# The third and fourth hidden tile of the first SwiGLU as a pair of seven block products

## The chip, the cores and the metric

The kernel runs on one core of a Trainium2 chip. The metric is device time in microseconds (us), the median over runs of the same kernel. In the profile, PE is TensorE (PEld its weight loads), DVE is VectorE, ACT is ScalarE, POOL is GpSimd, and SP is the engine whose queue issues the DMAs.

## The reference

One decoder layer on 512 tokens of width 1024, in float32. What the change touches is the first of its two SwiGLU blocks:

```
def swiglu(x, w_gate, w_up, w_down):
    return (jax.nn.silu(x @ w_gate) * (x @ w_up)) @ w_down

h = h + 0.5 * rms_norm(swiglu(rms_norm(h, ffn1_pre_g), ffn1_w_gate, ffn1_w_up, ffn1_w_down), ffn1_post_g)
u = rms_norm(h, mix_pre_g)          # then two token mixers: sparse latent attention and a gated recurrence
h = h + rms_norm(merged @ w_out, mix_post_g)
h = h + 0.5 * rms_norm(swiglu(...), ffn2_post_g)   # the second SwiGLU, its own weights
h = h + rms_norm(sigmoid(rms_norm(h) @ w_ple_gate) * (p @ w_ple_proj), ple_post_g)
```

The hidden width is 2816, that is 22 tiles of 128.

## The kernel before, in words

Activations lie with channels on the 128 partitions and the 512 tokens along the free dimension. Every float32 operand is split into a rounded part ("hi", cast by ACT) and the remainder ("lo", a subtraction on DVE), and every product is three matmuls: hi by hi, lo weight by hi, hi weight by lo. All matmuls are issued at line 259.

A SwiGLU (`ffn`) goes through its 22 hidden tiles in four groups, given by `GROUPS` as (first tile, tiles, how many of them are plain). The hidden tiles of a group are made first, and then all 8 output tiles get the group's share of the down product. A plain tile takes 24 matmuls for its gate and 24 for its up product, each over all 512 tokens. The other tiles go in pairs (`pair`, lines 512 to 590). There the product of a pair of weight tiles with the input is seen as a 2 by 2 block product (two tiles by two halves of the input channels, two halves of the channels by two halves of the tokens), and the gate and the up side each do it with seven block products instead of eight, in the order of `SEVEN` (lines 27 and 28):

```
SEVEN = (("a", True, "A11", "B11"), ("b", True, "A12", "B21"), ("a", False, "S2", "T2"), ("c", True, "S1", "T1"),
         ("a", False, "S3", "T3"), ("c", False, "S4", "B22"), ("a", False, "A22", "T4"))
```

The first name is the bank that is added into, the B's are quarters of the input, the A's of the weights, the S's sums of weight quarters. Each block product is 4 steps of 3 matmuls over 256 tokens. A pair's weight sums are made by POOL (lines 532 and 536) and DVE (533, 539, 565), and each is split by ACT (508) and DVE (509).

The T's are sums of input quarters. `input_sums` (lines 481 to 492) makes them once per SwiGLU. It is a generator of four steps; step k covers one of four channel blocks for all four T's: two scaled copies on ACT (486), four subtractions in a row on POOL (490), and a split of each result on ACT and DVE (199, 200, tile name T). Before, in the first SwiGLU, two steps are taken after tile 0, one after tile 1 and one after tile 2.

In the first SwiGLU tile 0 is special: `start` brings its weights and the input in together, and `start_scale` makes the factor R of the RMS norm (matmuls at 273 and 283, powers on POOL at 248, copies at 315). `hidden` then takes a product times R (382), a Silu on ACT (389), the product of both (391) and a split into hid_hi and hid_lo (199, 200).

Buffers come from pools: 5 raw weight tiles (`raw`), 6 split ones (`w`), 6 work tiles (`t`), and 6 PSUM banks that are handed out in turn (mm, pl, mm, pl, pt, po). A scheduler puts the instructions of each engine into a fixed order when the program is built, and each engine then works through its own queue in that order, waiting for what an instruction needs. A weight tile's DMA waits until its raw buffer is free.

Of the kernel before, what the change touches and what calls it, by code (L numbers as in the profile page):

```python
# [19 lines left out]
FT = DFF // P  # L20
EPS = 1e-6

GROUPS = ((0, 4, 4), (4, 6, 0), (10, 6, 0), (16, 6, 0))
INNER = 6


# [54 lines left out]
class Layer:  # L81
# [312 lines left out]
    def ffn(self, name, nxt, y, pool, spill=None, begin=None):  # L394
        nc, a = self.nc, self.a
        wg, wu, wd = (a[f"{name}_w_{s}"] for s in ("gate", "up", "down"))
        post = self.ghalf[f"{name}_post"]
        hid_hi = pool.tile([P, INNER, NT], F32R, name="hid_hi")
        hid_lo = pool.tile([P, INNER, NT], F32R, name="hid_lo")
        acc = self.accum(NT)  # L400
        for f0, nf, plain in GROUPS:
            first, last = f0 == 0, f0 + nf == FT
            j0 = 0
            if first and not begin:
                j0 = 3
                w = [self.first_weights(name, (wg[j], wu[j]), D, shift=SHIFT) for j in range(j0)]

                tags = iter(("mm", "mm", "pl", "pl", "pt", "po"))
                for cols in HALF:
                    for js in ((0, 1), (2,)):  # L410
                        banks = [self.bank(next(tags)) for _ in js]
                        ps = [(b[:, :256], b[:, 256:]) for b in banks]
                        self.mm3s([x for j, b in zip(js, ps) for x in zip(b, w[j])], self.hg_hi, self.hg_lo, KT, cols,
                                  shared=True)
                        for j, b in zip(js, ps):
                            self.hidden(hid_hi, hid_lo, j, *b, cols)
            elif first:
                j0 = 1
                w = begin[0](wg[0], wu[0])
                ps = self.bank("pl"), self.bank("pt")  # L420
                self.mm3s(list(zip(ps, w)), self.hg_hi, self.hg_lo, KT, FULL)
                begin[1]()
                self.hidden(hid_hi, hid_lo, 0, *ps, FULL)
            if first:
                sums = self.input_sums(f"{name}_pre", pool)
                next(sums)
                next(sums)
            for j in range(j0, plain):
                pg, pu = self.bank(), self.bank()
                self.mm3(pg, self.weight(wg[f0 + j], D), self.hg_hi, self.hg_lo, KT, FULL)  # L430
                self.mm3(pu, self.weight(wu[f0 + j], D), self.hg_hi, self.hg_lo, KT, FULL)
                self.hidden(hid_hi, hid_lo, j, pg, pu, FULL)
                next(sums, None)
            if first:
                for _ in sums:
                    pass
            for j in range(plain, nf, 2):
                self.pair(pool, [src[f0 + j:f0 + j + 2] for src in (wg, wu)], hid_hi, hid_lo, j)
            w = {}

            def parts(m, ps, cols, ks):
                if m not in w:
                    w[m] = self.weight(wd[m][:, f0 * P:(f0 + nf) * P], nf * P)
                for k in ks:
                    self.mm3_step(k, ps, w[m], hid_hi, hid_lo, nf, cols)

            def store(m, ps, cols):
                if first:
                    nc.scalar.copy(y[:, m, cols], ps)
                else:  # L450
                    nc.vector.tensor_tensor(y[:, m, cols], y[:, m, cols], ps, op=OP.add)
                if last:
                    self.square_sum(acc[:, cols], y[:, m, cols], m == 0, nc.vector if m == KT - 1 else nc.gpsimd)

            def product(m, cols):
                ps = self.bank()[:, :cols.stop - cols.start]
                parts(m, ps, cols, range(nf))
                store(m, ps, cols)


            early = 3
            ps = [self.bank() for _ in range(early)]
            for ks in (range(nf - 2), range(nf - 2, nf)):
                for m in range(early):
                    parts(m, ps[m], FULL, ks)
            for m in range(early):
                store(m, ps[m], FULL)
            if last:
                self.last_product(product, y, acc, post, nxt, TURN[name], spill, early, self.e)
                if begin:  # L470
                    self.ple_proj(pool)
            else:
                for m in range(early, KT):
                    product(m, FULL)
                if first and begin:
                    begin[2]()
# [799 lines left out]
```

## Time and profile before

| what | value |
|---|---|
| median of 3 runs | 1225.35 us (1225.05 to 1231.47) |
| the profiled execution | 1224.83 us |
| its span, first to last instruction | 1223.0 us |
| PE busy | 1185.8 us, 97% of the span |
| DVE busy | 896.9 us, 73% |
| ACT busy | 658.4 us, 54% |
| POOL busy | 521.5 us, 43% |

Times below are counted from the start of the span. A busy share is an average over all stages. For a change in one stage the stretch of that stage counts: here the first 85 us, in which the first group of the first SwiGLU runs.

### The profile page before, as it was taken

The page shows a single profiled execution, that of the slowest core. Times are in us where ns is not written, and L with a number is a line of the kernel's source. Part 1 is how long each engine was busy: PE and PEld are TensorE (multiplying, and loading weights), DVE is VectorE, ACT ScalarE, POOL GpSimd, SP SyncE. Part 2 cuts the span into 40 slices and gives each one's busy share as a digit, 9 for nine tenths or more (in the row PEclk, how much of TensorE's full clock was granted, in tenths as well). Part 3 has the DMA queues.
Part 4 walks back from the last instruction along what each step waited for, and adds up shares of the span by engine and source line. Part 5 has one row for each costly group of instructions (what it writes and reads, how often), then busy time and mean ns, then how long its engine had stood idle before and what let it go on. Part 6 is the DMA issues. An engine that isn't in the chain of part 4 may idle for free.

```text
span 1223.0 us, 20125 instructions
## 1 busy us (share of the span) xinstructions
PE 1185.8 (97%) x7580; PEld 1064.7 (87%) x7580; DVE 896.9 (73%) x1496; ACT 658.4 (54%) x1193; POOL 521.5 (43%) x521
## 2 busy tenths in 40 slices
PE   7999999999999999998999999999999999999997
PEld 6889899999999887787788878898899899899976
DVE  8769669669757479998576748387787587588396
ACT  6655435435645464564677755456655265255263
POOL 3525235235153213645657642363452252253364
PEclk9999999999999999999999999999999999999999
DMA  7242522522635212323222236322234233233131
GB/s 253 62 130 66 170 77 65 164 83 65 197 128 180 96 52 70 129 87 100 66 94 91 74 104 213 105 61 65 92 108 126 68 117 122 71 117 119 59 138 70
DMA packets 47058, 130.23 MB, mean 106 GB/s; under 512 B 5400, under 2 KB 9840, under 8 KB 46960
## 3 DMA queue, kind: packets, MB, share of 16 engines
q1 hardware_dynamic: 46960, 128.95, 32.2%
q8 instruction: 59, 0.97, 0.3%
q14 instruction: 39, 0.32, 0.1%
HBM read 118.16 MB, written 10.77 MB: 105 GB/s over the span
## 4 chain that ended last, share of the span: by engine, by line
PE 65%; DVE 16%; ACT 5%; POOL 5%; issue 5%; DMA 2%; SPq 0%; DVEq 0%; POOLq 0%; ACTq 0%
PE mm L259 24%; PE pl L259 18%; PE pt L259 8%; PE po L259 8%; DVE sc L706 2%; DVE w L178 2%; DVE w L509 1%; DVE small L705 1%; DVE hg_lo L306 1%; PE po L755 1%; DMA g<-gate_d 1%; DVE h L360 1%; DVE z L358 1%; POOL t L490 1%; POOL acc L299 1%
## 5 line engine op out<-in xcount | busy, mean ns | idle before, releaser
L259 PE MATMUL mm<-hg_hi,w 128*128 128x512 f32 (+1 forms) x984 | 268.1, 355 | 3.3 <-ACT hg_hi L199 1.5
L259 PEld LDWEIGHTS mm<-hg_hi,w 128*128 128x128 f32 x984 | 171.0, 188 | 27.8 <-ACT hg_hi L199 1.7
L176 ACT ACTIVATE w<-raw 128x1024 fp32r<-128x1024 f32 (+5 forms) x146 | 131.9, 910 | 84.6 <-PE pl L259 26.0
L259 PE MATMUL mm<-hg_lo,w 128*128 128x512 f32 (+1 forms) x492 | 173.4, 353 | 0.1
L178 DVE TENSOR_TENSOR w<-raw,w 128x1024 fp32r<-128x1024 f32 (+5 forms) x132 | 141.3, 1075 | 40.4 <-ACT w L176 40.3
L532 POOL TENSOR_TENSOR s<-raw 128x512 f32<-128x512 f32 x36 | 50.8, 1411 | 238.3 <-DMA raw<-ffn_w_gate 164.3
L509 DVE TENSOR_TENSOR w<-raw,w 128x1024 fp32r<-128x1024 f32 (+1 forms) x108 | 132.0, 1236 | 7.2 <-ACT w L508 6.5
L508 ACT ACTIVATE w<-raw 128x1024 fp32r<-128x1024 f32 (+1 forms) x108 | 95.3, 911 | 45.4 <-PE mm L259 15.0
L259 PE MATMUL pl<-hg_hi,w 128*128 128x256 f32 (+1 forms) x520 | 111.6, 307 | 5.0 <-ACT w L176 5.0
L259 PEld LDWEIGHTS mm<-hg_lo,w 128*128 128x128 f32 x492 | 92.3, 188 | 12.0 <-DVE hg_lo L306 0.3
L299 POOL TENSOR_TENSOR acc<-acc,sq 128x256 f32<-128x256 f32 x78 | 68.0, 879 | 72.3 <-ACT sq L298 70.9
L259 PEld LDWEIGHTS pl<-hg_hi,w 128*128 128x128 f32 x520 | 84.2, 191 | 10.0 <-ACT w L176 5.0
L259 PE MATMUL pl<-hg_lo,w 128*128 128x256 f32 (+1 forms) x260 | 79.1, 304 | 0.7 <-DVE hg_lo L306 0.7
L259 PE MATMUL pl<-T,w 128*128 128x256 f32 x576 | 75.5, 281 | 4.1 <-ACT sq L548 4.1
L259 PE MATMUL pl<-hid_hi,w 128*128 128x512 f32 (+1 forms) x276 | 76.6, 362 | 0.0
L259 PE MATMUL mm<-T,w 128*128 128x256 f32 x576 | 74.9, 279 | 1.5 <-ACT sq L548 1.5
L562 POOL TENSOR_TENSOR t<-t,acc 128x256 f32<-128x256 f32 x36 | 43.1, 1198 | 75.8 <-ACT t L561 75.8
L259 PEld LDWEIGHTS pl<-T,w 128*128 128x128 f32 x576 | 70.9, 190 | 4.7 <-ACT sq L548 4.7
L533 DVE TENSOR_TENSOR s<-s,raw 128x512 f32<-128x512 f32 x36 | 39.0, 1084 | 47.9 <-POOL s L532 47.9
L259 PE MATMUL mm<-hid_hi,w 128*128 128x512 f32 (+1 forms) x268 | 73.4, 361 | 0.0
L259 PEld LDWEIGHTS mm<-T,w 128*128 128x128 f32 x576 | 70.4, 189 | 1.7 <-ACT sq L548 1.7
L508 ACT ACTIVATE w<-s 128x1024 fp32r<-128x1024 f32 x36 | 38.3, 1064 | 56.8 <-PE pl L259 18.7
(361 smaller groups left out, 3009.8 us busy)
## 6 DMA issues: line engine op xcount, KB each, us to landing
raw<-ffn_w_gate SPq DMA_DIRECT2D x43, 512.0 KB, 3.9
raw<-ffn_w_up SPq DMA_DIRECT2D x43, 512.0 KB, 4.1
raw<-ffn_w_down SPq DMA_DIRECT2D x48, 384.0 KB, 3.7
raw<-w_gates SPq DMA_DIRECT2D x16, 512.0 KB, 3.6
raw<-ffn_w_down SPq DMA_DIRECT2D x16, 256.0 KB, 2.7
gate_d<-t SPq DMA_DIRECT2D x16, 256.0 KB, 2.1
raw<-w_br SPq DMA_DIRECT2D x8, 512.0 KB, 3.5
raw<-w_out SPq DMA_DIRECT2D x8, 512.0 KB, 4.0
```

What stands on the lines that cost most here:

```text
L176: hi = nc.scalar.activation(w[:, 0, c], raw[:, c], AF.Copy)
L178: lo = eng.tensor_tensor(w[:, 1, c], raw[:, c], w[:, 0, c].bitcast(F32), op=OP.subtract)
L259: i = self.nc.tensor.matmul(*args, **kw)
L299: eng.tensor_tensor(acc[:, c:c + 256], acc[:, c:c + 256], sq, op=OP.add)
L306: lo = nc.vector.scalar_tensor_tensor(self.hg_lo[:, k, cols], self.h[:, k, cols], g, self.hg_hi[:, k, cols].bitcast(F32), op0=OP.mult, op1 ...
L358: nc.vector.scalar_tensor_tensor(z, y[:, k, c], g[:, k:k + 1], bc, op0=OP.mult, op1=OP.mult)
L508: self.nc.scalar.activation(w[:, 0], raw, AF.Copy)
L509: eng.tensor_tensor(w[:, 1], raw, w[:, 0].bitcast(F32), op=OP.subtract)
L532: pool_.tensor_tensor(s[:, low], r[1][:, low], r[1][:, high], op=OP.add)
L533: dve.tensor_tensor(s[:, high], s[:, low], r[0][:, low], op=OP.subtract)
L562: pool_.tensor_tensor(o2[:, two], o2[:, two], k["P5"], op=OP.add)
L706: nc.vector.match_replace(sc, best, sc, TAKEN)
```

## The change

`GROUPS` becomes a table by SwiGLU. The second SwiGLU keeps its numbers. In the first one, two of the first group's four tiles are plain instead of four, so tiles 2 and 3 go as a pair, and all four steps of `input_sums` are taken after tile 0 instead of two. One more line moves every line number behind it by one in the changed kernel.

```
-GROUPS = ((0, 4, 4), (4, 6, 0), (10, 6, 0), (16, 6, 0))
+GROUPS = {"ffn1": ((0, 4, 2), (4, 6, 0), (10, 6, 0), (16, 6, 0)),
+          "ffn2": ((0, 4, 4), (4, 6, 0), (10, 6, 0), (16, 6, 0))}
...
-        for f0, nf, plain in GROUPS:
+        for f0, nf, plain in GROUPS[name]:
...
                 sums = self.input_sums(f"{name}_pre", pool)
-                next(sums)
-                next(sums)
+                for _ in range(2 if plain > 2 else 4):
+                    next(sums)
```

The scheduler makes a new order of it. On DVE, between the weights of tile 1 and the hidden values of tile 0, there stood before (w is a split weight, hid_lo and T the remainders of a hidden tile and of an input sum):

```order
L178 TENSOR_TENSOR w<-raw,w 128x1024
L250 TENSOR_SCALAR e<-small_263 128x2
L178 TENSOR_TENSOR w<-raw,w 128x1024 x2
L178 TENSOR_TENSOR w<-raw,w 128x512
L382 TENSOR_TENSOR t<-pl,R 128x512
L391 TENSOR_TENSOR t<-pt,t 128x512
L200 TENSOR_TENSOR hid_lo<-t,hid_hi 128x512
L200 TENSOR_TENSOR T_278<-t,T_278 128x256
```

and now, in the changed kernel, whose lines 383, 392, 510, 534 and 540 are lines 382, 391, 509, 533 and 539 of before:

```order
L540 TENSOR_TENSOR raw<-raw,s 128x512
L510 TENSOR_TENSOR w<-raw,w 128x1024
L510 TENSOR_TENSOR w<-s,w 128x1024
L534 TENSOR_TENSOR s<-s,raw 128x512
L540 TENSOR_TENSOR raw<-raw,s 128x512
L510 TENSOR_TENSOR w<-s,w 128x1024
L510 TENSOR_TENSOR w<-raw,w 128x1024
L383 TENSOR_TENSOR t<-pl,R 128x512
L392 TENSOR_TENSOR t<-pt,t 128x512
L510 TENSOR_TENSOR w<-raw,w 128x1024
L201 TENSOR_TENSOR hid_lo<-t,hid_hi 128x512
L201 TENSOR_TENSOR T_278<-t,T_278 128x256
```

The pair's weight sums and five of its six whole remainders now stand ahead of tile 0's first hidden instruction (382 before, 383 now).

On POOL, after the sums of squares of the start, there stood before (r is the factor of the norm, t<-t the subtractions of `input_sums`):

```order
L341 TENSOR_TENSOR acc_218<-acc_218,t 128x256 x7
L248 TENSOR_TENSOR r<-small_253,mhalf 128x2
L248 TENSOR_TENSOR r<-small_263,mhalf 128x2
L490 TENSOR_TENSOR t<-t 128x256 x16
L532 TENSOR_TENSOR s<-raw 128x512
```

and now:

```order
L342 TENSOR_TENSOR acc_218<-acc_218,t 128x256 x7
L533 TENSOR_TENSOR s<-raw 128x512
L249 TENSOR_TENSOR r<-small_253,mhalf 128x2
L537 TENSOR_TENSOR raw<-raw 128x512
L249 TENSOR_TENSOR r<-small_263,mhalf 128x2
L533 TENSOR_TENSOR s<-raw 128x512
L537 TENSOR_TENSOR raw<-raw 128x512
L491 TENSOR_TENSOR t<-t 128x256 x16
L597 TENSOR_TENSOR t<-t,R 128x512
```

Four weight sums of the new pair have come ahead of the 16 subtractions, two of them ahead of the second power.

On PE, where tile 1 ends and tile 2 began, there stood 512-wide rows of tile 2, which need hg (the input) and a split weight alone:

```order
L259 MATMUL pl<-hg_hi,w 128x512 x2
L259 MATMUL pl<-hg_lo,w 128x512
L259 MATMUL mm<-hg_hi,w 128x512 x2
L259 MATMUL mm<-hg_lo,w 128x512
L259 MATMUL mm<-hg_hi,w 128x512 x2
```

and now, after the first two block products of the pair (48 rows of 256 that read hg), come those that read the input sums, T_279 being T2 of the list above and T_278 T1:

```order
L260 MATMUL po<-hg_lo,w 128x256
L260 MATMUL mm<-T_279,w 128x256 x3
L260 MATMUL pl<-T_279,w 128x256 x3
L260 MATMUL mm<-T_279,w 128x256 x2
L260 MATMUL pl<-T_279,w 128x256 x2
L260 MATMUL mm<-T_279,w 128x256
L260 MATMUL pl<-T_279,w 128x256
L260 MATMUL mm<-T_279,w 128x256 x2
L260 MATMUL pl<-T_279,w 128x256 x2
L260 MATMUL mm<-T_279,w 128x256
L260 MATMUL pl<-T_279,w 128x256
L260 MATMUL mm<-T_278,w 128x256 x12
```

So PE's third block product is the first that reads an input sum, and it is queued in steps of one channel block, with nothing between them that doesn't need a sum.

## Rows read from the trace of the kernel before

**Rows 1.** Page, busy time: engine, us (share of the span), instructions.
```profile
PE 1185.8 (97%) x7580; PEld 1064.7 (87%) x7580; DVE 896.9 (73%) x1496; ACT 658.4 (54%) x1193; POOL 521.5 (43%) x521
```

**Rows 2.** Chain of waits, 28 to 100 us: start, us, what.
```profile
34.15 5.44 PE mm L259 x24
...
50.47 5.44 PE po L259 x24
...
74.95 2.72 PE pl L259 x12
...
84.07 1.36 PE mm L259 x12
```

**Rows 3.** Timeline of PE at tile 2: start, us, instruction, count.
```profile
33.99 0.39 PE L259 MATMUL mm<-hg_hi,w 128*128 128x512 f32 x1
```

**Rows 4.** Timeline of ACT, 24 to 34 us; in brackets the idle time before and its releaser.
```profile
25.25 1.06 ACT L176 ACTIVATE w<-raw 128x1024 fp32r<-128x1024 f32 x1 [2.84 <-DMA raw<-ffn_w_up]
28.02 0.37 ACT L315 COPY R<-hg 128x256 f32<-128x256 f32 x1 [1.71 <-PE hg L283]
...
30.57 1.28 ACT L389 ACT_TABLE_LOAD   x1 [1.14 <-DVE t L382]
...
32.41 1.32 ACT L486 ACTIVATE t<-h,vecs 128x512 f32<-128x512 f32 x2
```

**Rows 5.** Timeline of POOL, 20 to 75 us.
```profile
22.62 2.90 POOL L248 TENSOR_TENSOR r<-small,mhalf 128x2 f32<-128x2 f32 x2 [5.30 <-DVE small L247]
33.26 7.44 POOL L490 TENSOR_TENSOR t<-t 128x256 f32<-128x256 f32 x8 [7.74 <-ACT t L486]
...
47.46 3.92 POOL L490 TENSOR_TENSOR t<-t 128x256 f32<-128x256 f32 x4 [1.67 <-ACT t L486]
57.68 1.28 POOL L532 TENSOR_TENSOR s<-raw 128x512 f32<-128x512 f32 x1 [6.29 <-DMA raw<-ffn_w_gate]
59.04 1.80 POOL L536 TENSOR_TENSOR raw<-raw 128x512 f32<-128x512 f32 x1
```

**Rows 6.** Timeline of DVE, 28 to 45 us.
```profile
29.81 0.69 DVE L382 TENSOR_TENSOR t<-pl,R 128x512 f32<-128x512 f32 x1
...
38.81 2.84 DVE L200 TENSOR_TENSOR T<-t,T 128x256 fp32r<-128x256 f32 x5
```

**Rows 7.** Groups by line and shape, 20 to 60 us: count, busy us, mean ns, idle before.
```profile
L490 POOL TENSOR_TENSOR t<-t 128x256 f32<-128x256 f32 x16 | 15.0, 960 | 10.9 <-ACT t L486 10.5
...
L200 DVE TENSOR_TENSOR T<-t,T 128x256 fp32r<-128x256 f32 x16 | 9.3, 635 | 0.5 <-ACT T L199 0.5
L178 DVE TENSOR_TENSOR w<-raw,w 128x1024 fp32r<-128x1024 f32 x6 | 7.2, 1213 | 0.2 <-ACT w L176 0.2
...
L199 ACT ACTIVATE T<-t 128x256 fp32r<-128x256 f32 x16 | 6.5, 413 | 4.3 <-POOL t L490 4.2
...
L178 DVE TENSOR_TENSOR w<-raw,w 128x512 fp32r<-128x512 f32 x6 | 6.2, 1032 | 1.6 <-ACT w L176 1.6
...
L200 DVE TENSOR_TENSOR hid_lo<-t,hid_hi 128x512 fp32r<-128x512 f32 x3 | 3.5, 1176 | 1.0 <-ACT hid_hi L199 1.0
```

**Rows 8.** PE's waits at a pair's third product, in the timeline.
```profile
123.67 1.65 PE L259 MATMUL mm<-T,w 128*128 128x256 f32 x12 [1.53 <-ACT sq L548]
...
906.73 1.65 PE L259 MATMUL pl<-T,w 128*128 128x256 f32 x12 [2.18 <-ACT sq L548]
...
927.98 1.67 PE L259 MATMUL pl<-T,w 128*128 128x256 f32 x12 [1.92 <-ACT sq L548]
```

**Rows 9.** Windows: us, busy us (count) of PE, PEld, DVE, ACT, POOL; PEclk, DMA, GB/s.
```profile
124.00:126.00 2.00, 2.00 (x20) 2.00 (x19) 2.00 (x6) 1.25 (x3) 0.00 (x0) 1.00 0.87 232
...
928.00:930.00 2.00, 2.00 (x15) 2.00 (x16) 2.00 (x6) 1.15 (x3) 0.00 (x0) 0.87 0.77 206
930.00:932.00 2.00, 2.00 (x11) 2.00 (x10) 2.00 (x4) 1.71 (x4) 0.00 (x0) 0.50 0.63 196
932.00:934.00 2.00, 2.00 (x15) 2.00 (x15) 0.96 (x2) 0.37 (x1) 0.00 (x0) 0.78 0.87 260
```

## The prediction

> **What bounds the kernel now.** I read the page first. PE is busy 97% of the span and DVE 73% [rows 1], so what counts is how many matmuls there are and where PE waits. The chain of waits says which of the two it is in the stretch of the change: from 34 to 56 us it runs through PE alone, 24 matmuls of 512 columns in 5.44 us, four times over (the first and the last of the four stand in [rows 2]). That is 0.2267 us for each, with no gap. Further on, 12 matmuls of 256 columns take 1.36 us, 0.1133 us each, exactly half [rows 2]. So less arithmetic is less time there, as long as PE finds its operands ready. The timelines of ACT, POOL and DVE then show what makes the operands. POOL is done with the norm at 25.5 us and idle for 7.74 us, until the first of the scaled copies on ACT is made, which starts at 32.41 [rows 4, 5]. Those copies stand in ACT's queue behind the Silu of tile 0, which waits for DVE's product with R [rows 4, 6]. In the kernel before nobody waits for the input sums: POOL ends the last one at 51.4 [rows 5], and the first pair comes only behind the down product, which ends at 77.7 [rows 2].
>
> **What goes.** Tiles 2 and 3 take 96 matmuls of 512 columns, 96 x 0.2267 = 21.76 us. The pair takes 2 sides x 7 products x 12 = 168 of 256 columns, 168 x 0.1133 = 19.04 us. PE's work falls by 2.72 us. That is the whole possible gain in this stage.
>
> **What comes, and what it delays.** PE is through with tile 1 at 33.99 [rows 3], and tile 1 itself is unchanged. The first two block products need only the input and the first weight of each side, and those are cast ahead of the fourth weight tile, which lands at 25.25 [rows 4], with 1.21 for a remainder [rows 7]. So they run to 33.99 + 48 x 0.1133 = 39.4. The third needs T2 from all four steps of the input sums. I follow the chain to it.
>
> The up side's sum on POOL (L532) now stands behind the two powers with a subtraction between them: 22.62 + 1.45 + 1.80 + 1.45 = 27.3 [rows 5]. Its data, the fourth weight tile, landed at 25.25 as before [rows 4]. The sum ends at 27.3 + 1.28 = 28.6 [rows 5]. DVE then adds the other quarter (0.69, as any of its 512-column steps [rows 6]), to 29.3. ACT casts this sum and then the gate side's third weight, 1.06 each [rows 4], to 31.4, and copies R twice (0.37 each [rows 4]), to 32.1. DVE's remainder of that third weight takes 1.21 [rows 7], to 32.6, and tile 0's product with R 0.69 [rows 6], to 33.3. Before it was over at 30.5. From its end to the first scaled copy before took 1.91 us (the table load, 1.28, and the Silu) and from there to POOL's first subtraction 0.85 [rows 4 to 6]. So POOL starts at about 36.1, not 33.26.
>
> POOL does 8 subtractions in 7.44 us, 0.93 each [rows 5], over all 16 the mean is 0.96 [rows 7]. T2 of the last step is the 14th: 36.1 + 14 x 0.94 = 49.2. Cast (0.41) and remainder (0.64) [rows 7] bring 50.3.
>
> DVE's queue says a little more. Behind tile 0's Silu ACT makes two scaled copies (1.2 us) and then casts the up side's third weight (1.06 [rows 4]), to 37.5. From there DVE has, up to the 14th remainder of a sum: that weight 1.21, the remainder of tile 0's hidden values 1.18, the two halves of the seventh weight and one down weight, 1.03 each [rows 7], tile 1's two products 0.69 each [rows 6], one short addition (0.41, as a cast of its size), and 14 remainders. Five of these took 2.84 us [rows 6], where five of the mean 0.635 [rows 7] would be 3.2: neighbours overlap a little. At 0.55 each they make 7.7. The list adds up to 15.0, and I take 14.6 for the overlap: the end is 52.1. I take the later of the two. Four matmuls follow on it, 0.45, so the first four block products are done at 52.55. Without a wait their 96 matmuls would be done at 33.99 + 10.88 = 44.87. PE waits 7.7 us.
>
> The ends of this term: with POOL starting at 33.26 as before, and DVE keeping pace, the last T2 is there at 33.26 + 13.2 + 1.05 = 47.5, and the wait is 3.1 (47.95 less 44.87). With every remainder held back by a POOL instruction, see the third rival, it is 10.8.
>
> After that I see no further wait in the group. The last weights are split by about 44.4 (the first part of the list above), the copies of the banks are hidden by down matmuls of tiles 0 and 1 that are queued between, and the hidden values of tile 3 are not needed until 18 other down matmuls, 4.1 us, are done. The down weights' DMAs come later, since the pair holds raw tiles until 44.4, but PE wants the second of them only after 60 (52.55 and the 72 matmuls left of the pair).
>
> **The clock.** PE's granted clock fell once it had stood still: after the wait of 1.92 us before 927.98 the windows show 0.87, 0.50 and 0.78, that is 1.2 instead of 2.4 GHz for 3.4 us, at a cost of half of that, 1.7 [rows 8, 9]. After the wait of 1.53 us before 123.67 it stayed at 1.00 [rows 9]. Between 39.4 and about 48.5 PE would have three bursts of six matmuls, 0.7 us each, so I count one fall; what of it lies behind the restart can cost nothing, or twice that row's 1.7; I take 1.7. [...]
>
> **Behind the group** the instructions on all engines keep their kinds, and nearly all their order. PE gets to the second group some 5 to 7 us later, which gives its first weights more time than they lose. I count 0, within the 1.53 of the wait before 123.67 [rows 8] either way.
>
> **The sum.** 7.7 - 2.72 + 1.7 = +6.7 us against the profiled execution's 1224.83 (span 1223.0 and 1.8 around it): 1231.5. The median of the runs shown, 1225.35, is 0.5 higher than that execution, which I leave out.
>
> **Rivals.**
>
> First, the sums keep pace better than I reckon: POOL starts at 33.26, PE waits 3.1 us, and the clock stays up as it did at 123.67 [rows 9]. For it: POOL has 7.74 us of idle time ahead of the sums [rows 5], and the added two sums and two differences need about 6.2 of them (2 x 1.28 + 2 x 1.80). Against it: the copies that start the sums wait for DVE, not for POOL. It gives 1224.83 + 3.1 - 2.7 = 1225.2, no change. I give it 0.20.
>
> Second, and on the other side: the wait comes, but later waits are spared. At three places the third product of a pair waits for a copy on ACT, 1.53, 2.18 and 1.92 us, and one of them brings the slow clock, 1.7 [rows 8, 9]. The first group now takes 18 banks in turn instead of 14, so all later pairs of both SwiGLUs meet other banks of the six, and in the first SwiGLU DVE could get ahead of a PE that is late. If all four go, that is 7.3 us: 1231.5 - 7.3 = 1224.2, not slower. It decides once more than 6.7 us are spared. Against it: those waits come out of ACT's queue behind weight casts, and those follow PE's release of the weight buffers, so they move along with PE. I give it 0.07.
>
> Third, the preparation is heavier than reckoned, since DVE and POOL slow each other: a remainder of an input sum took 0.635 us on average [rows 7]. If each waits for the subtraction beside it to end, one of each takes 0.96 + 0.41 = 1.37 us (0.41 for an undisturbed one, as the cast of that size [rows 7]), and the 14th is done at 36.1 + 14 x 1.37 = 55.3, with the 0.45 behind it 10.8 us after 44.87. With two falls of the clock, 3.4, it gives 1224.83 + 10.8 - 2.7 + 3.4 = 1236.3. Five remainders in 2.84 us beside running subtractions speak against it [rows 6]. The Trainium skill, SBUF — State Buffer, section "Who interferes with whom", has this as a rule: a VectorE instruction with two SBUF inputs and a GpSimd one that reads SBUF share a port, and the later one blocks for the whole of the other. By that rule, the trace agrees in part: the remainders are stretched, not serialised. I give it 0.15.
>
> **How the numbers follow.** My forecast, a wait of 5 to 10 us in the third product, has 0.58; its own range is 1228 to 1235. What a measurement can tell from no change is 0.5%, 6.1 us, so slower begins at 1231.5, just where the forecast lies: half of it, 0.29, counts as slower, with the third rival 0.44, and a little for falls of the clock elsewhere, 0.46. Within 0.5%: the other 0.29, the first rival 0.20, most of the second: 0.52. Faster by over 6.1 us would need the gain of 2.72 and several spared waits without the new one: 0.02. The range, from the first rival to just short of the third: 1225 to 1236.
>
> **What would show it.** Right: a wait of PE between 39 and 52 us, ended by ACT or DVE on T or by POOL's subtractions; POOL's 16 subtractions in one run of about 15 us starting near 36; a window of clock 0.5 near 50; the last matmul of the first group's down product near 84 instead of 77.7 [rows 2]; all later stages at the same lengths. Wrong: the subtractions starting by 33 or taking turns with PE so that it waits under 3 us; a new wait in the first two products or for a weight; or the three waits of rows 8 gone.

## The result: slower, and by more than predicted

The changed kernel takes 1242.35 us (median of 4 runs, 1241.29 to 1245.12), the kernel before 1227.45 (4 runs beside it): 1.0119 times as long, 95% interval 1.0099 to 1.0138. The forecast was 1231.5, in a range of 1225 to 1236. It is slower by more than 0.5%, the loss more than twice the one forecast. The profiled executions are 1241.45 and 1224.83 us long, their spans 1239.7 and 1223.0. Of the 16.7 us between the spans 12.2 are lost in the first group: its last matmul ended at 74.95 + 2.72 = 77.7 [rows 2], and now at 89.9. The 1224.83 is one of the shortest executions of its kernel (1223.52 to 1233.34 in the 23 runs beside e11 below), and between the medians lie 14.9 us.

Page of the changed kernel, busy time [rows 1]:

```profile
PE 1192.5 (96%) x7652; PEld 1070.7 (86%) x7652; DVE 909.8 (73%) x1508; ACT 661.8 (53%) x1205; POOL 537.8 (43%) x529
```

PE's busy time has risen by 6.7 us, though its work has fallen. The chain of waits, which was PE alone from 34 to 56 us [rows 2], now runs through DVE and ACT until 54:

```profile
36.21 0.61 DVE t L383
...
47.80 1.73 DVE T L201 x2
...
50.67 1.93 DVE T L201 x5
...
54.07 3.35 PE mm L260 x14
57.42 2.23 PE pl L260 x13
59.99 0.70 PE pt L260 x3
```

The timeline of PE in the new pair (start, us, instruction, count, and in brackets the wait before it and who ended it). Its place is that of tile 2, which began at 33.99 before [rows 3]:

```profile
34.35 0.40 PE L260 MATMUL mm<-hg_hi,w 128*128 128x256 f32 x2
...
36.87 0.50 PE L260 MATMUL pl<-hg_hi,w 128*128 128x256 f32 x2 [0.83 <-DVE t L383]
...
42.33 0.50 PE L260 MATMUL mm<-T,w 128*128 128x256 f32 x2 [1.19 <-ACT T L200]
43.84 0.38 PE L260 MATMUL mm<-T,w 128*128 128x256 f32 x1 [1.01 <-DVE T L201]
...
46.09 0.79 PE L260 MATMUL mm<-T,w 128*128 128x256 f32 x2 [1.50 <-ACT T L200]
...
49.58 0.58 PE L260 MATMUL mm<-T,w 128*128 128x256 f32 x1 [2.28 <-DVE T L201]
...
54.07 3.35 PE L260 MATMUL mm<-T,w 128*128 128x256 f32 x14 [0.67 <-DVE t L383]
57.22 2.43 PE L260 MATMUL pl<-T,w 128*128 128x256 f32 x13
...
59.82 0.63 PE L260 MATMUL pt<-hid_hi,w 128*128 128x512 f32 x2
...
89.90 0.81 PE L159 MATMUL pl<-t,rel 32*8 32x384 f32 x2
```

The reader is to see that PE doesn't stand still once, but goes on in drops of two to four matmuls from 42 to 54 us. The first four block products are done at 59.8. Tile 1 ended at 34.35 here, so without a wait they would be done at 34.35 + 10.88 = 45.2: 14.6 us are lost. The part from 59.8 to 89.9 takes 30.1 us. By the prediction's own figures for what is left, 72 matmuls of the pair (8.16) and the down product of before (77.7 - 33.99 - 21.76 = 21.9), it should take 30.1. So the 2.72 us of saved work are real, and nothing else is lost in this group.

Windows of the changed kernel (busy us and count of PE, PEld, DVE, ACT, POOL; then the granted clock, DMA share, GB/s):

```profile
44.00:48.00 4.00, 1.81 (x8) 1.30 (x8) 4.00 (x5) 3.58 (x9) 3.92 (x5) 0.65 0.08 11
48.00:52.00 4.00, 2.02 (x6) 1.43 (x6) 4.00 (x7) 2.30 (x5) 2.64 (x4) 0.50 0.47 132
52.00:56.00 4.00, 2.73 (x11) 2.44 (x12) 4.00 (x7) 1.87 (x6) 2.86 (x4) 0.50 0.16 54
56.00:60.00 4.00, 4.00 (x24) 4.00 (x24) 2.09 (x6) 1.37 (x4) 0.00 (x0) 0.64 0.00 0
```

DVE is busy for all of the 12 us from 44 to 56, POOL for most of it, and the clock is at its lower level, 1.2 GHz. The 30 matmuls from 54.07 to 59.82 took 5.75 us and would take 3.4 at 0.1133 each, so by this estimate the clock accounts for 2.4 of the 14.6 us, and waiting for 12.2. The slow matmuls ahead of 54.07 count as waiting, since a further wait followed each drop of them. (The two 12.2 are different sums: 12.2 of waiting, 2.4 of the clock and the 0.36 by which tile 1 ended later, less the 2.72 saved, make the 12.2 by which the group ends later.)

The timelines of POOL [rows 5] and DVE [rows 6], and two groups of 20 to 60 us [rows 7]:

```profile
19.70 4.28 POOL L533 TENSOR_TENSOR s<-raw 128x512 f32<-128x512 f32 x1 [2.02 <-DMA raw<-ffn_w_gate]
...
28.12 1.74 POOL L533 TENSOR_TENSOR s<-raw 128x512 f32<-128x512 f32 x1
...
38.17 11.95 POOL L491 TENSOR_TENSOR t<-t 128x256 f32<-128x256 f32 x12 [6.08 <-ACT t L487]
51.48 3.46 POOL L491 TENSOR_TENSOR t<-t 128x256 f32<-128x256 f32 x4 [1.36 <-DVE T L201]
```

```profile
20.48 2.35 DVE L179 TENSOR_TENSOR w<-raw,w 128x1024 fp32r<-128x1024 f32 x2
...
22.82 2.25 DVE L510 TENSOR_TENSOR w<-raw,w 128x1024 fp32r<-128x1024 f32 x1
...
28.64 2.31 DVE L510 TENSOR_TENSOR w<-s,w 128x1024 fp32r<-128x1024 f32 x1
30.87 1.77 DVE L534 TENSOR_TENSOR s<-s,raw 128x512 f32<-128x512 f32 x1
...
36.13 0.68 DVE L383 TENSOR_TENSOR t<-pl,R 128x512 f32<-128x512 f32 x1
...
39.69 1.23 DVE L510 TENSOR_TENSOR w<-raw,w 128x1024 fp32r<-128x1024 f32 x1 [1.49 <-ACT w L509]
...
41.98 3.55 DVE L201 TENSOR_TENSOR T<-t,T 128x256 fp32r<-128x256 f32 x4
...
56.07 0.74 DVE L201 TENSOR_TENSOR T<-t,T 128x256 fp32r<-128x256 f32 x2
```

```profile
L201 DVE TENSOR_TENSOR T<-t,T 128x256 fp32r<-128x256 f32 x16 | 10.6, 712 | 0.0
...
L491 POOL TENSOR_TENSOR t<-t 128x256 f32<-128x256 f32 x16 | 15.1, 967 | 7.8 <-ACT t L487 6.1 <-DVE T L201 1.4
```

POOL's first sum of weights takes 4.28 us instead of the 1.28 of [rows 5]; it begins shortly before two undisturbed remainders on DVE (2.35 us for both) and ends inside a third, which takes 2.25 instead of 1.2. Instructions of DVE that run beside POOL are up to 2.6 times as long (1.77 instead of 0.69). The hidden values of tile 0, which start the sums, begin at 36.13 instead of 29.81 [rows 6]; the prediction had 32.6 from the new order alone, and the other 3.5 us come of this.

Behind the first group this profile is 4.5 us longer. By PE's timeline the second group takes 95.3 us instead of 92.5 and the product behind the two mixers 48.4 instead of 46.4; the rest keeps its length within 0.3 in sum, though not in its parts (the second group of the second SwiGLU takes 95.5 instead of 97.0). In the second group two waits, 0.51 and 1.93 us, stand where one of 1.53 stood, and the 12 matmuls behind the longer take 2.77 instead of 1.65 us [rows 8]:

```profile
137.18 2.77 PE L260 MATMUL pt<-T,w 128*128 128x256 f32 x12 [1.93 <-ACT sq L549]
```

### The profile page after: what moved, and what is told of

The parts are those of the page before. It is cut to its first block, busy times and chain, and to the rows that moved or that the text cites. A ratio compares the mean times of both kernels' runs of the same rounds, so it can differ in the third digit from the quotient of the medians.

```text
span 1239.7 us, 20305 instructions
## 1 busy us (share of the span) xinstructions
PE 1192.5 (96%) x7652; PEld 1070.7 (86%) x7652; DVE 909.8 (73%) x1508; ACT 661.8 (53%) x1205; POOL 537.8 (43%) x529
## 4 chain that ended last, share of the span: by engine, by line
PE 61%; DVE 17%; POOL 6%; ACT 6%; issue 6%; DMA 2%; SPq 0%; DVEq 0%; POOLq 0%; ACTq 0%
PE mm L260 23%; PE pl L260 16%; PE po L260 7%; PE pt L260 7%; DVE w L179 2%; DVE sc L707 2%; DVE w L510 2%; DVE small L706 1%; DVE hg_lo L307 1%; PE po L756 1%; DMA g<-gate_d 1%; POOL acc L300 1%; DVE z L359 1%; ACT w L509 1%; DVE h L361 1%
## 5 line engine op out<-in xcount | busy, mean ns | idle before, releaser
L177 ACT ACTIVATE w<-raw 128x1024 fp32r<-128x1024 f32 (+4 forms) x142 | 127.8, 906 | 80.8 <-PE pl L260 26.9
L179 DVE TENSOR_TENSOR w<-raw,w 128x1024 fp32r<-128x1024 f32 (+4 forms) x128 | 137.1, 1076 | 37.2 <-ACT w L177 37.1
L533 POOL TENSOR_TENSOR s<-raw 128x512 f32<-128x512 f32 x38 | 58.5, 1540 | 238.5 <-DMA raw<-ffn_w_gate 149.2
L510 DVE TENSOR_TENSOR w<-raw,w 128x1024 fp32r<-128x1024 f32 (+1 forms) x114 | 138.7, 1230 | 7.9 <-ACT w L509 7.9
L509 ACT ACTIVATE w<-raw 128x1024 fp32r<-128x1024 f32 (+1 forms) x114 | 100.3, 910 | 50.1 <-PE mm L260 17.8
L260 PE MATMUL pl<-hg_hi,w 128*128 128x256 f32 (+1 forms) x512 | 106.9, 302 | 6.5 <-ACT w L177 5.1
L260 PE MATMUL mm<-T,w 128*128 128x256 f32 x624 | 85.6, 286 | 8.2 <-DVE T L201 4.0
L260 PEld LDWEIGHTS mm<-T,w 128*128 128x128 f32 x624 | 79.2, 194 | 10.2 <-DVE T L201 4.8
L260 PE MATMUL pl<-T,w 128*128 128x256 f32 x624 | 83.5, 283 | 0.6 <-ACT sq L549 0.6
L260 PEld LDWEIGHTS pl<-T,w 128*128 128x128 f32 x624 | 78.2, 192 | 1.0 <-ACT sq L549 1.0
L260 PE MATMUL pl<-hid_hi,w 128*128 128x512 f32 (+1 forms) x280 | 77.7, 362 | 0.0
```

What stands on the lines that cost most here:

```text
L177: hi = nc.scalar.activation(w[:, 0, c], raw[:, c], AF.Copy)
L179: lo = eng.tensor_tensor(w[:, 1, c], raw[:, c], w[:, 0, c].bitcast(F32), op=OP.subtract)
L260: i = self.nc.tensor.matmul(*args, **kw)
L509: self.nc.scalar.activation(w[:, 0], raw, AF.Copy)
L510: eng.tensor_tensor(w[:, 1], raw, w[:, 0].bitcast(F32), op=OP.subtract)
L533: pool_.tensor_tensor(s[:, low], r[1][:, low], r[1][:, high], op=OP.add)
```

## The experiments

"Tile 1" is the end of tile 1, where the pair (or tile 2) begins, and "first group" the end of its down product, both in the profiled execution of each kernel; the ratio is that of the kernel's runs to those of the kernel before on the same chip, with its 95% interval. Tile 1 runs ahead of the pair, and its end moves by up to 1.2 us between profiles, most of it in the first 23 us (in e4 it is later by the change itself). One profile stands behind each row, so differences of about 1 us between rows say little.

| run | tile 1, us | first group, us | median, us | ratio |
|---|---|---|---|---|
| before | 33.99 | 77.7 | 1227.45 | |
| changed | 34.35 | 89.9 | 1242.35 | 1.0119 [1.0099, 1.0138] |
| e1 sums moved, no pair | 35.08 | 79.6 | 1228.55 | 1.0009 [0.9994, 1.0024] |
| e2 pair that reads no sums | 34.94 | 86.5 | 1239.32 | 1.0103 [1.0086, 1.0120] |
| e3 old turn of the banks | 34.25 | 89.2 | 1239.77 | 1.0103 [1.0086, 1.0120] |
| e4 sums ahead of tile 0 | 37.44 | 87.3 | 1237.28 | 1.0085 [1.0070, 1.0100] |
| e5 sums' remainders on ACT | 34.36 | 88.6 | 1238.59 | 1.0095 [1.0067, 1.0123] |
| e6 no subtractions on POOL | 34.01 | 83.3 | 1233.26 | 1.0058 [1.0037, 1.0080] |
| e7 PE kept busy | 35.02 | 92.8 | 1243.94 | 1.0131 [1.0106, 1.0155] |
| e8 no weight sums on POOL | 35.01 | 87.7 | 1240.54 | 1.0094 [1.0074, 1.0114] |
| e9 neither on POOL | 34.86 | 80.9 | 1231.43 | 1.0016 [1.0002, 1.0030] |
| e10 both on DVE | 33.93 | 83.1 | 1233.42 | 1.0042 [1.0025, 1.0059] |
| e11 e10, old turn | 34.68 | 83.7 | 1232.32 | 1.0037 [1.0021, 1.0054] |
| e12 e11, two sum steps earlier | 35.08 | 85.6 | 1232.56 | 1.0029 [1.0011, 1.0048] |

**e1.** All four steps of the sums behind tile 0, all four tiles plain.

```
-GROUPS = {"ffn1": ((0, 4, 2), ...
+GROUPS = {"ffn1": ((0, 4, 4), ...
-                for _ in range(2 if plain > 2 else 4):
+                for _ in range(4 if begin else 2):
```

> All four steps of the input sums behind tile 0, but tiles 2 and 3 stay plain. Theory A (the loss is PE's wait for the input sums in the pair's third product): no product reads a sum before 78 us, so nothing is lost: 1227 us, within 3. Theory B (the loss is the pair's weight preparation, which holds up DVE, POOL and tile 0's hidden values): the same, 1227. If moving the sums alone costs (they stand ahead of tile 1's hidden values on ACT and DVE, and the down product waits for those): over 1232.

No change in the time that can be measured. The first group ends 1.9 us later in this profile; 1.1 of them lie ahead of tile 1's end, and 0.55 are a new wait for the remainder of a hidden tile (at 64.58). So moving the sums costs little by itself; it is the pair that needs them, or what the pair adds.

**e2.** The pair's products take quarters of the input where they took sums; the sums are still made.

```
+        if self.blind and name[0] == "T":
+            name = {"1": "B11", "2": "B12", "3": "B21", "4": "B22"}[name[1]]
```

> The changed kernel, but the new pair's products read quarters of the input in place of the four input sums (that part of the result is left wrong); the sums are still made behind tile 0 for the later pairs. Theory A: the third product no longer waits, the clock stays up, and the pair gives its 2.7 us: PE ends the first group at 75 to 77 us, and the kernel takes 1225 us, or up to 1229 if the later stages keep the 4.5 us that they lost. Theory B: PE still waits 5 us or more in the first group, 1235 or more.

Only 3.4 of the 12.2 us come back. PE's waits in that kernel, whose lines from 200 on stand one or some lines further down:

```profile
42.55 0.50 PE L261 MATMUL mm<-hg_hi,w 128*128 128x256 f32 x2 [0.86 <-ACT sq L553]
48.02 0.65 PE L261 MATMUL mm<-hg_hi,w 128*128 128x256 f32 x2 [2.48 <-ACT z L553]
54.66 0.50 PE L261 MATMUL mm<-hg_hi,w 128*128 128x256 f32 x2 [2.04 <-DVE t L384]
```

With no sum to wait for, PE waits for banks that ACT's copies and DVE's product of tile 1 have to give back, and these stand in queues behind the sums. So the wait for T2 is only where the loss shows first; the theory on which the prediction rests falls in good part. What is left is that the queues themselves are too long.

**e3.** Two banks are passed over behind the pair, so that later pairs meet the banks of before.

```
+            for _ in range(2 if first and begin else 0):
+                next(self.ring)
```

> The changed kernel with two more banks passed over behind the pair, so that all later products meet the same banks as in the kernel before. Theory C (what is lost behind the first group, 4.5 of the 16.7 us between the two profiles, comes of the shifted turn of the banks): 1238 us, with the waits at the pairs' third products as in the kernel before. If the turn is not it: 1242, within 2.

The second group takes 92.5 us again, with one wait as at 123.67 [rows 8], and no fall of the clock:

```profile
135.32 1.65 PE L260 MATMUL mm<-T,w 128*128 128x256 f32 x12 [1.53 <-ACT sq L551]
```

The time doesn't settle it, as the intervals of this kernel and the changed one overlap.

**e4.** The four steps of the sums are written ahead of tile 0's hidden values.

```
+                sums = self.input_sums(f"{name}_pre", pool)
+                for _ in range(4):
+                    next(sums)
                 self.hidden(hid_hi, hid_lo, 0, *ps, FULL)
```

> The changed kernel with the four steps of the input sums written ahead of tile 0's hidden values instead of behind them, so that ACT's scaled copies need not stand behind the Silu. Theory A: POOL's subtractions start near 28 instead of 38, the wait shrinks to 3 to 6 us and the clock loss with it: 1231 to 1237. Theory B: the work on DVE is the same and so is the time, 1240 or more.

The drops in the pair become one wait, for the bank of tile 0:

```profile
46.34 0.80 PE L260 MATMUL pl<-hg_hi,w 128*128 128x256 f32 x2 [5.92 <-DVE t L383]
```

POOL's subtractions begin at 17.32 here, and another 3.1 us are lost ahead of the pair, as tile 1 ends at 37.44. The result lies between what the two theories gave: the order decides where PE waits, and only 2.6 us of how long.

**e5.** ACT instead of DVE makes the low parts of the sums.

```
-                self.split(self.T[i][:, 0, k, :], self.T[i][:, 1, k, :], o)
+                nc.scalar.activation(self.T[i][:, 0, k, :], o, AF.Copy)
+                nc.scalar.activation(self.T[i][:, 1, k, :], o, AF.Copy)
```

> ACT makes a second copy in place of each of DVE's 16 remainders of the input sums (the low parts of the sums are wrong by that). DVE loses 16 x about 0.7 = 11 us of its queue, ACT gains 16 x about 0.3 = 5 us. Theory 'DVE is full': PE's wait nearly goes, the first group's down product ends near 78 (76 to 81) instead of 89.9, median 1228 to 1233. Theory 'POOL's chain is late': POOL's subtractions still start near 37 and end near 53, so PE waits 7 us or more, group end 85 or later, median 1237 or more.

Neither came out whole: the first group ends 1.3 us earlier. DVE has room now, but ACT is full, 4.00 of 4.00 us, and POOL beside the idle DVE takes 0.69 us for a subtraction (its timeline):

```profile
48.00:52.00 4.00, 0.84 (x5) 0.54 (x4) 0.52 (x1) 4.00 (x12) 3.16 (x5) 0.50 0.46 148
```

```profile
48.55 2.77 POOL L491 TENSOR_TENSOR t<-t 128x256 f32<-128x256 f32 x4 [1.08 <-ACT t L487]
```

So the load can't be carried over to ACT. And "DVE is full" was too simple, since POOL's pace depends on what DVE does; the next run shows the same of DVE's on POOL's.

**e6.** POOL's 16 subtractions are left out.

```
-                nc.gpsimd.tensor_tensor(o, x, z, op=OP.subtract)
                 self.split(self.T[i][:, 0, k, :], self.T[i][:, 1, k, :], o)
```

> POOL's 16 subtractions of the input sums are left out, and each sum is split straight from a scaled copy (the sums are wrong by that). DVE's remainders stay, but nothing on POOL stretches them: 16 x (0.71 - 0.41) = 5 us less in DVE's queue. Theory 'POOL's chain is late': the wait goes, group end 76 to 79, median 1228 to 1231. Theory 'DVE is full': it goes in part only, group end 82 to 86, median 1232 to 1237.

6.6 us come back, part of the wait, as the theory of the full DVE gave it. The same 16 remainders take 0.415 us each instead of 0.712, eight in a row 0.345:

```profile
42.32 2.76 DVE L201 TENSOR_TENSOR T<-t,T 128x256 fp32r<-128x256 f32 x8
```

**e7.** Matmuls that nobody reads keep PE busy ahead of the third product.

```
+            if n == 2 and self.fill:
+                spare = self.bank("hg")[:, :256]
+                for f in range(self.fill):
+                    self.matmul(spare, sides[0][3]["A12"][:, 0, c], self.hg_hi[:, f % 8, HALF[0]], ...
```

> 105 matmuls of 256 columns into a bank that nobody reads, between the second and the third product of the first pair: 11.9 us of PE at full clock, inside the time in which PE waits. The result is unchanged. If the slow clock is part of the loss, it stays at 1.00 through the pair and the first group ends 2.4 us or so earlier than 89.9, near 87.5, median near 1240. If the slow clock costs nothing (the stretch was bound by operands anyway), the end is 89.9 or later, and the median not below 1242.

```profile
52.00:56.00 4.00, 3.24 (x27) 2.84 (x25) 4.00 (x6) 1.98 (x6) 3.12 (x4) 1.00 0.13 44
56.00:60.00 4.00, 3.20 (x19) 3.20 (x20) 2.95 (x8) 2.09 (x5) 0.00 (x0) 0.73 0.01 2
```

The clock stayed at 1.00 until 56 and then fell all the same, and the group ends 2.9 us later. That is what was expected if the slow clock costs nothing, but it isn't a clean test, since the third product now starts at 53.56 instead of 42.33. What the clock alone costs stays an estimate, the 2.4 us read from the rows; no run shows it.

**e8.** POOL's sums and differences of the first pair's weights are left out.

```
-            pool_.tensor_tensor(s[:, low], r[1][:, low], r[1][:, high], op=OP.add)
-            pool_.tensor_tensor(r[1][:, low], r[0][:, low], r[1][:, low], op=OP.subtract)
```

> In the first pair, POOL's two sums and two differences of weights are left out; DVE's and ACT's instructions there stay, on the raw weights (the pair's products are wrong by that). POOL's 16 subtractions of the input sums stay. Theory 'POOL and DVE hold each other up': DVE's remainders of the pair's weights take 1.2 us again instead of 2.3, tile 0's product with R ends near 33 instead of 36.8, the subtractions start near 34 to 35, and the first group ends 2 to 4 us earlier, 86 to 88, median 1238 to 1240. Theory 'the work on DVE and ACT alone is too much': the end stays at 89 to 90, median 1241 to 1243.

The raw tile is split in place of the missing sums. 2.2 us come back in the profile, or 2.8 counted from tile 1's end, within what the theory gave; by the time the kernel can't be told from the changed one. DVE's remainders of these weights are undisturbed, and POOL begins at 35.27 instead of 38.17:

```profile
27.76 2.35 DVE L510 TENSOR_TENSOR w<-raw,w 128x1024 fp32r<-128x1024 f32 x2
```

**e9.** Both are left out.

> Both left out, POOL's sums and differences of weights and its 16 subtractions of the input sums; all of DVE's, ACT's and PE's instructions stay (sums and products wrong by that). Theory 'POOL and DVE hold each other up': nothing stretches DVE's remainders between 20 and 58 us, the first group ends at 76 to 80 (89.9 - 6.6 of the subtractions alone - 3 for the weights' sums, and the clock up), median 1226 to 1231. Theory 'the work on DVE and ACT alone is too much': the end stays above 82, near the 83.3 without the subtractions, median 1232 or more.

9.0 us come back, and 6.6 + 2.2 is 8.8 (from tile 1's end 9.6, and 6.3 + 2.8): the two add up. The longest wait in the pair is 1.12 us, and the clock stays up:

```profile
44.00:48.00 4.00, 2.81 (x20) 2.12 (x18) 3.37 (x7) 4.00 (x11) 0.00 (x0) 1.00 0.44 132
```

The other 3.2 us against the kernel before, or 5.9 against the end with the saving, come without these instructions of POOL; 0.9 of them lie ahead of tile 1's end. In this window ACT is the full one.

**e10.** POOL's instructions of both kinds run on DVE; the arithmetic is that of the changed kernel.

```
-                nc.gpsimd.tensor_tensor(o, x, z, op=OP.subtract)
+                nc.vector.tensor_tensor(o, x, z, op=OP.subtract)
-            pool_.tensor_tensor(s[:, low], ...
+            (dve if begin else pool_).tensor_tensor(s[:, low], ...
```

> The same arithmetic as the changed kernel, but the first pair's weight sums and differences and all 16 subtractions of the input sums run on DVE instead of POOL, 4 x 0.68 + 16 x 0.35 = 8.3 us more in DVE's queue. Theory 'POOL and DVE hold each other up': DVE gets about as much back, 16 x (0.71 - 0.35) + 4 x 1.1 = 10.2 us, as its remainders are not stretched any more; the end of the first group is 86 to 90, median 1238 to 1243, no later than the changed kernel. Theory 'DVE's own work is too much': DVE's queue is 8 us longer, the end 95 or later, median 1247 or more.

This decides it between the two theories. With 20 instructions more in its queue, DVE is done earlier, the first group ends 6.8 us earlier (6.4 from tile 1's end), beyond what was expected, and the interval of the ratio lies clear of the changed kernel's. Groups of 20 to 60 us:

```profile
L491 DVE TENSOR_TENSOR t<-t 128x256 f32<-128x256 f32 x16 | 6.3, 417 | 0.1
L201 DVE TENSOR_TENSOR T<-t,T 128x256 fp32r<-128x256 f32 x16 | 6.1, 414 | 0.0
...
L510 DVE TENSOR_TENSOR w<-s,w 128x1024 fp32r<-128x1024 f32 x2 | 2.4, 1211 | 0.0
```

Subtractions and remainders of the sums together take 12.4 us on DVE. In the changed kernel the remainders alone took 10.6 there, and POOL's subtractions 15.1 beside them. DVE's timeline, from the pair's last whole weight to the 14th remainder of the sums:

```profile
36.62 1.23 DVE L510 TENSOR_TENSOR w<-raw,w 128x1024 fp32r<-128x1024 f32 x1 [0.47 <-ACT w L509]
...
50.09 1.08 DVE L201 TENSOR_TENSOR T<-t,T 128x256 fp32r<-128x256 f32 x3
```

The 14th is the first of these three and ends at 50.5. So this list takes 13.9 us with 12 subtractions in it, where it took 16.8 without them in the changed kernel (39.69 to 56.5). That it also begins 3.1 us earlier is not all due to the missing POOL: the scheduler made another order here, in which tile 0's product with R (at 30.25) stands ahead of two of the weights' remainders that it stood behind. How much of the 6.8 us the order gives was not tested. What is left of PE's wait:

```profile
42.94 0.51 PE L260 MATMUL mm<-T,w 128*128 128x256 f32 x2 [2.48 <-ACT T L200]
```

**e11 and e12.** e10 with the two banks passed over as in e3, and e12 in addition with two of the sums' steps ahead of tile 0's hidden values.

> The previous version (POOL's work of the first pair and of the input sums on DVE) with the two extra banks passed over, so that all later pairs meet the banks they met before the change. The result is unchanged. If the two causes add up (POOL and DVE holding each other up in the first group, the turn of the banks behind it): first group's end near 83, second group back from 97 to 93 us, median 1229 to 1231, still not below the kernel before, since PE still waits 4 us at the sums. If the later loss isn't from the turn: median stays at 1233.

> As the run before it, and two of the four steps of the input sums are written ahead of tile 0's hidden values, so that T2's first half is made while PE is still on tile 1. The result is unchanged. If lateness of the first sums is what is left of the wait: first group's end 79 to 82, median 1226 to 1229, within the noise of the kernel before. If DVE's queue is full whichever way it is ordered: the end stays at 83 or comes later, since tile 0's banks are given back late, median 1229 to 1233.

Neither can be told from e10 by its time, and neither beats the kernel before. In e11 the second group takes 94.6 us instead of e10's 97.0, in e12 92.4. The earlier sums don't help the first group: DVE and ACT have the same work in another order.

## Why the prediction was wrong

**Right:** the saved 2.72 us; the place and the kind of the loss, PE between 39 and 54 us, waiting for ACT and DVE on T; POOL's pace, 0.94 expected and 0.967 measured; the first and the second rival out (the later waits of [rows 8], 5.63 us in sum, are five now, 0.51, 1.93, 2.25, 0.32 and 0.31, 5.32 in sum).

**The size.** Of the 10.9 us by which the forecast missed the median, 2.6 are its start from the execution of 1224.83, where the median of the kernel before is 1227.45. The change itself was forecast at 6.7 and measured at 14.9.

**The step that failed first: "The sum ends at 27.3 + 1.28 = 28.6".** The pair's preparation was priced by rows in which the other engine stood idle or worked on two columns: 1.28 for POOL's sum, 1.21 for DVE's remainder, 0.69 for its addition. In the changed kernel they run side by side: a sum takes 4.28 us, two remainders 2.25 and 2.31, an addition 1.77. Rows of the kernel before had shown it: remainders of 128x512, 0.69 in e9, stand in [rows 7] at 1.03 and 1.18. Tile 0's product with R was to end at 33.3 and ended at 36.8; 1.3 of these 3.5 us are regained, as ACT loads its table ahead of that product's end now. POOL was to begin at 36.1 and began at 38.2, and DVE's list, which was to begin at 37.5, began at 39.69. That is 2.2 us, and e8 returns 2.2 to 2.8. The prediction's own sign of being wrong, a new wait in the first two products, came with it: 0.83 us at 36.87, for the bank that this product gives back.

**The second: "At 0.55 each they make 7.7".** The five remainders in 2.84 us [rows 6], 38.81 to 41.65, were taken as the pace of a queue beside running subtractions, against the mean of 0.635 [rows 7]. But POOL's first eight subtractions ended at 33.26 + 7.44 = 40.70 [rows 5], and it was idle until its next line in the trace of before:

```profile
41.84 3.96 POOL L490 TENSOR_TENSOR t<-t 128x256 f32<-128x256 f32 x4 [1.14 <-ACT t L486]
```

So a third of those 2.84 us had no neighbour. Measured, 16 took 0.712 each. The list was to take 14.6 us, and from 39.69 to the 14th remainder's end, 56.07 + 0.41, it took 16.8. So it ends 2.2 + 2.2 = 4.4 us later than the 52.1 of the prediction, about the difference between the wait forecast, 7.7, and measured, 12.2. PE's last wait was not ended by that remainder, though, but by another instruction of the same list, tile 1's product with R (53.33), for a bank, and 30 matmuls stood behind it instead of the four counted.

**The third rival** had this mechanism and 0.15. Its wait of 10.8 us (10.9 by its own sum) came near the 12.2 partly by luck, as two errors went opposite ways. It was priced too high for each pair of instructions, 0.96 + 0.41 = 1.37, since the 0.96 already held the remainder beside it: POOL takes 0.69 alone (e5) and DVE 0.345 (e6), together 1.04, and the measured 0.967 is about that sum. They nearly take turns. And it was placed too early, since it left out the same thing ahead of tile 0. The Trainium skill, SBUF — State Buffer, section "Who interferes with whom", has it that of a VectorE instruction with two SBUF inputs and a GpSimd one that reads SBUF the later blocks until the other is done; the prediction read the five remainders as evidence against it, and the measured sum is evidence for it.

**The clock** fell once, as counted, but for nearly 14 us instead of 3.4. Most of that lay where PE waited anyway; by the estimate above 2.4 us were paid, 1.7 forecast.

**"Behind the group I count 0"**, within 1.53, missed this profile, which has 4.5 us more there. That the change costs them is not shown: the span less the end of the first group is 1145.3 us in the profile of before, 1149.8 in that of the changed kernel, and 1142.0 to 1151.4 among all of them; in e1, whose time can't be told from the kernel before, it is 1150.8. For 2.8 of the 4.5, the second group, the new turn of the banks is a possible cause: with the turn of before it took 92.4 to 94.6 us in five profiles (before, e1, e3, e11, e12), with the new turn 94.1 to 97.0 in nine. The ranges overlap and no time confirms it. The 2.0 behind the mixers stay open; that stage varies from 46.4 to 48.4 us among all these profiles.

**Not settled either:** what ACT's full queue costs by itself. In e9 and e10 it is what PE waits for at the longest waits, but no run took work from ACT alone. So the cause is shown for the 6.6 to 9.0 us that come back without POOL's instructions (e6, e9); the rest of the loss in the group stays open.

## What to carry to other kernels

Work that is given to POOL because DVE is full isn't free for DVE when both read SBUF: look at what a DVE instruction takes in the trace beside a POOL instruction and without one, and if the two durations add up, let DVE do it (here 12.4 us on DVE in place of 10.6 there and 15.1 on POOL, and 6.8 us off the stage, part of them perhaps by the new order). Price an instruction that is moved by a row with the neighbours that it will have, not by one with idle neighbours. And if PE waits in drops on operands of two engines that have no gap, count each engine's whole queue up to the last operand, before reordering anything: e4 and e12 moved the wait and kept most of it.

## What the runs showed of the hardware

- A POOL subtraction of 128x256 took 0.69 us beside an idle DVE (four in a row, e5) and 0.967 beside DVE's remainders; these took 0.345 in a row of eight, and 0.712 beside POOL. A POOL sum of 128x512 took 1.28 us alone and 4.28 beside DVE's instructions, most of them remainders of 128x1024. The Trainium skill, Perfetto Trace Analysis, section "Optimizing Scalar/DVE Operations", says that offloading between GpSimd and VectorE might not help, since they share a port; e10 agrees, with 6.8 us.
- The granted clock fell to 0.50 in the changed kernel between 45 and 46 us, after waits of 0.83, 1.19 and 1.01 us and inside one of 1.50, and stayed at 1.00 in e9, with waits of 0.98, 0.33 and 1.12 us in the same stretch. The longest wait alone doesn't tell: in e4 the clock fell at 24 us, where six waits of 0.28 to 0.69 us lay between 15 and 24 us.
